# Half of the first layer's output product as seven block products instead of eight, with the weight sums formed by transfers

## The chip, the cores and the metric

The kernel runs on one core of one Trainium2 chip. The metric is device time in microseconds (us): the time of one execution, median of several runs. Each kernel was also executed once under the hardware profiler, and all instruction times below come from that one execution.

The engines are named as the profile names them. PE is the matrix engine and PEld its load of the stationary operand; DVE and ACT are the vector and scalar engines; POOL is the general engine, which here issues some transfers and does a little arithmetic; SP issues most transfers. Each engine works through its own instructions strictly in program order.

## The reference

Four residual layers over 256 tokens of width 1024, in float32. Layers 0 and 3 are of kind A, layer 1 of kind B (attention), layer 2 of kind C (pooling). Layer 0 is what the change touches:

```python
h = rms_norm(x, norm_gain[i])
proj = h @ w_in                      # 1024 -> 3 * 2048
u, v, z = proj[..., :2048], rms_norm(proj[..., 2048:4096], v_gain), proj[..., 4096:]
mixed = einsum('gij,bcjgd->bcigd', tril(w_s), v) + b_s   # 128-token chunks, 8 groups
y = u * mixed * silu(z)              # 256 x 2048
x = x + y @ w_out                    # 2048 -> 1024, the output product
```

The change concerns the first 1024 rows of `w_out`, and with them the first 1024 columns of `y`, in layer 0 alone.

## The kernel before

**Precision.** Every float32 operand is split in a high part, rounded to the format that PE takes at full rate, and the low rest. A product is three matmuls (`mm3`, lines 87 to 89): high by high, high by low, low by high, added up in one PSUM bank. The high part is made by ACT (`hi_of`, L92), the low part by DVE (`lo_of`, L95).

**Weights.** All weights lie in DRAM as one stream of units in the order of use. A unit is 256 rows by 512 columns, 512 KB. Unit u is loaded by SP (`load_units`, L177) into a raw buffer, split by ACT and DVE into one of seven pairs of buffers (`W_BUFS = 7`), and used by PE. There are four raw buffers of the tag `wr`; in the last layer `wx`, `wy` and `xs` serve as three more (`raw_place`). A raw buffer can be loaded again when the low part of its unit has been made.

**The order by hand.** `step(kk)` stands behind each half of a unit. It calls `tick()`, which runs the small tasks that are due, and then places the splitting of the unit five ahead (`AHEAD = 5`): the high part at the first half (kk = 0), the low part at the second (kk = 1). So a task that falls due at kk = 0 is placed ahead of the next ACT split, and one that falls due at kk = 1 ahead of the next DVE split. A tick has no time of its own: it sets only the order in each engine's program. What holds an engine up are the waits for data and for buffers.

**Layer 0.** Units 0 to 15 give v (four stages of 512 columns), units 16 to 47 alternate z and u (z0, u0, ..., z3, u3, four units each), units 48 to 63 are the output product `wo`. After each u stage `y_task` multiplies on DVE (`sz` L669, `yy` L674); two and four ticks later PE transposes the two token halves (`yp`, L682) through a single PSUM buffer, ACT and DVE split them (`y00h`, `y00l` and so on). The output product (`proj_out`) keeps four accumulators, two token halves t by two column halves n. One unit meets both token halves: 12 matmuls of 512 columns. At the end DVE adds the accumulators to `x` (L551).

**PSUM.** The big products take banks in turn from a ring of four (`pp`); a bank can be written again when its last reader is done.

**Seven products in layer 3.** For three of its four z/u pairs, layer 3 already replaces eight products of 512x512 blocks by seven (Strassen's scheme in Winograd's form). Each block product is 4 k-tiles by three matmuls with 128 tokens; its two units serve one token half only, so a unit gives 6 matmuls instead of 12. The sums of weight quarters are made in DRAM by POOL's transfers (`sums_of_quarters`, L188 for copies, L186 for adding ones; 16 transfers of 512 KB for one block), 19 of them placed in layer 0, 16 in layer 1 and 13 in layer 2 (`JOBS`). The sums of the activations' quarters are made on DVE and ACT (`sums_task`, L699 and L704) early in layer 3.

Of the kernel before, what the change touches and what calls it, by code (L numbers as in the profile page):

```python
# [10 lines left out]
F32 = mybir.dt.float32  # L11
# [3 lines left out]
ALU = mybir.AluOpType  # L15
PSUM = bass.MemoryType.PSUM

P = 128
# [25 lines left out]
LAST_AHEAD = 3  # L44
WARM = 17
FILL = 4
SEVEN = (0, 2, 3)
JOBS = (19, 16)


@with_exitstack
def hybrid_trunk_kernel(ctx, tc, x, wts, norm_gainT, a_v_gain, a_wsT, a_bsT, b_gl, b_gv, c_scaleT,
# [89 lines left out]


    seq = list(range(n_units))
    sums = {(n, j): dp.tile([4, P, UNIT], F32, name=f"sums{n}{j}") for n in SEVEN for j in range(2)}

    def seven_units(n):

        return n_units - 48 + 8 * n + (8 if n == 3 else 0)

    for n in reversed(SEVEN):
        z = seven_units(n)
        seq[z:z + 8] = [e[j] for e in (((n, 0, 0), (n, 0, 1)), (z, z + 1), (z + 6, z + 7), ((n, 3, 0), (n, 3, 1)),
                                       (z + 2, z + 3), ((n, 2, 0), (n, 2, 1)), ((n, 1, 0), (n, 1, 1)))
                        for j in range(2)]
    n_seq = len(seq)

    raw_users = {"wr": [-1] * RAW_BUFS, "xs": [-1], "wx": [-1], "wy": [-1]}

    def raw_place(i):  # L160

        return ("wr", "wr", "wx", "wr", "wy", "wr", "xs")[i % 7] if i >= n_units - 48 else "wr"

    def load_free():

# [22 lines left out]
                nc.gpsimd.dma_start(dst, src, max_dma_last_dim=UNIT)  # L188
            yield every

    def sum_jobs(n):

        z = seven_units(n)
        both = range(2)
        jobs = [(sums[n, j][i], wts[z + 2 * q + j], add) for i, q, add in
                ((0, 0, False), (2, 2, False), (0, 2, True), (2, 3, True)) for j in both]
        jobs += [(sums[n, j][3], sums[n, j][0], False) for j in both]
        jobs += [(sums[n, j][1], wts[z + 2 + j], False) for j in both]  # L200
        jobs += [(sums[n, j][3], wts[z + 6 + j], True) for j in both]
        jobs += [(sums[n, j][1], sums[n, j][3], True) for j in both]
        return jobs

    def split_hi(n):
# [316 lines left out]
    def proj_out(layer, nkt, yT, k0=0):  # L522


        acc = [[[(slice(0, HALF), pp(f"wo{layer}_{t}{n}"))] for n in range(2)] for t in range(2)]
        if layer == DEPTH - 1:

            acc[1][1] = [(slice(0, S), acc[1][1][0][1][:, :S]), (slice(S, HALF), atp(f"wo{layer}_b")[:, :S])]
        jt = (nkt - TAIL) // 2
        for j in range(k0 // 2, jt):  # L530
            for n in range(2):
                w = next_unit()
                for kk in range(2):
                    k = 2 * j + kk
                    for t in range(2):
                        for cs, o in acc[t][n]:
                            mm3(o, yT(k, t), (w[0][:, kk, cs], w[1][:, kk, cs]), k == k0, False)
                    step(kk, AHEAD if nkt == 16 else LAST_AHEAD)
        tail = [(j, n, next_unit()) for j in range(jt, nkt // 2) for n in range(2)]
        if nkt == 16:  # L540
            tail.sort(key=lambda e: e[1])
        ss = [tiny(2, f"ss{layer}_{t}") for t in range(2)]
        for t in range(2):
            for i, (j, n, w) in enumerate(tail):
                for cs, o in acc[t][n]:
                    for kk in range(2):
                        k = 2 * j + kk
                        mm3(o, yT(k, t), (w[0][:, kk, cs], w[1][:, kk, cs]), False, k == nkt - 1)
# [22 lines left out]
                tick()  # L571


    def load_a(layer, j):
# [13 lines left out]
    def layer_a(layer, consts, pl, mid):  # L588
# [98 lines left out]
                    yield 1  # L687
            done.add(("y", layer, n))


        if layer == DEPTH - 1:
            smh, sml = pair(pl, [P, 4, 4, P], "sm", f"sm{layer}", 1)

        def sums_task():
            q = {}
            for k, t in ((1, 1), (0, 1), (0, 0), (1, 0)):
                d = q[k, t] = tmp("sz", f"sq{layer}{k}{t}", 4).rearrange("p (k c) -> p k c", c=P)
                hh, hl = (a[:, 4 * k:4 * k + 4, t * P:(t + 1) * P].bitcast(F32) for a in hcur)
                nc.vector.tensor_tensor(d, hh, hl, op=ALU.add)  # L699
                yield 1  # L700
            a11, a12, a21, a22 = q[0, 0], q[1, 0], q[0, 1], q[1, 1]
            for i, (d, a, b, op) in enumerate(((a22, a21, a22, ALU.subtract), (a21, a11, a21, ALU.subtract),
                                               (a11, a22, a11, ALU.subtract), (a12, a12, a11, ALU.add))):
                nc.vector.tensor_tensor(d, a, b, op=op)  # L704
                hi_of(smh[:, i], d)
                yield 1
                lo_of(sml[:, i], d, smh[:, i])
                yield 1
            done.add(("sums", layer))

        S_A21_A22, S_A11_A21, S_REST, S_A12_REST = range(4)

        def seven_products(n):

            need(("sums", layer))

            def sm(i):
                return lambda k: (smh[:, i, k], sml[:, i, k])

            def product(o, a, first):  # L720
                for j in range(2):
                    w = next_unit()
                    for kk in range(2):
                        k = 2 * j + kk
                        mm3(o, a(k), (w[0][:, kk], w[1][:, kk]), first and k == 0, k == 3)
                        step(kk, due=kk == 1)

            def minus(o, name):
                d = tmp("vv", name, 2)
# [50 lines left out]
        for n in range(4):  # L780
            spawn(v_task(n, first if first and n == 0 else
                         proj_tok(f"v{layer}{n}", skew=layer if n == 0 else None)))
            if layer == DEPTH - 1 and n == 0:
                spawn(sums_task(), 4)
        def get(k, t):
            need(("y", layer, k // 4))
            sl = slice(t * P, (t + 1) * P)
            return yT[k // 4][0][:, k % 4, sl], yT[k // 4][1][:, k % 4, sl]

        if layer == 0:  # L790
            spawn(sums_of_quarters(jobs[:JOBS[0]], 4, 6))
        for n in range(4):
            if layer == DEPTH - 1 and n == 3:
                proj_half(layer, KT, get)
            if layer == DEPTH - 1 and n in SEVEN:
# [12 lines left out]


    def load_b():  # L810
# [20 lines left out]
    def layer_b(layer, consts, pl):  # L831
# [215 lines left out]
        for hp in range(NHEAD // 2):  # L1047
            for g in range(NG):
                spawn(qk_task(hp, g, proj_tok(f"qk{hp}{g}", skew=layer if hp == 0 and g == 0 else None)))
                if hp == 0 and g == 0:  # L1050
                    spawn(sums_of_quarters(jobs[JOBS[0]:sum(JOBS)], 10, 5))
                    gate(0)
                    gate(1)
            o = proj_tok(f"v01{hp}")
# [24 lines left out]
    def layer_c(layer, pl):  # L1079
# [103 lines left out]

        a, b, c, d = C_ORDER
        spawn(gate_tok(a, proj_tok(f"cz{a}", skew=layer)))
        spawn(sums_of_quarters(jobs[sum(JOBS):], 7, 4))
# [19 lines left out]


    box = {}
    jobs = [e for n in SEVEN for e in sum_jobs(n)]

    def after_ws():
        spawn(load_b())
# [36 lines left out]
def _weight_stream(a_w_in, a_w_out, b_w_in, b_w_out, c_w_in, c_w_grp, c_w_out):  # L1249
    parts = []  # L1250

    def layer_a(j):
        w = a_w_in[j]
        for n in range(4):
            parts.append(_units(w[:, 2048 + n * HALF:2048 + (n + 1) * HALF]))
        out_units = _out_units(a_w_out[j])
        for n in range(4):
            if j == 1 and n == 3:
                parts.append(out_units[:8])
# [105 lines left out]
```

## Time and profile before

| what | value |
|---|---|
| median of 3 runs | 828.72 us (828.41 to 828.74) |
| the profiled execution's own time | 828.51 us |
| its span, first to last instruction | 826.8 us |
| PE busy | 821.1 us (99%) |
| DVE busy | 581.4 us (70%) |
| ACT busy | 514.9 us (62%) |
| POOL busy | 83.5 us (10%) |
| moved by transfers | 184.21 MB, mean 223 GB/s |

The span is 1.7 us shorter than the execution's time; the rest lies before the first and after the last instruction. Busy time counts an engine from start to end of its instructions, overlaps once. A matmul's end is modelled, so its price is read from the distance between two starts. In the rows of the timeline the first number is the start, the second the duration, both in us, then engine, line, operation, written and read names, shape and count; in square brackets the idle time before and what ended it.

### The profile page before, as it was taken

Reading aid. Unit: us, or ns where it says so; the run is one execution under the profiler, and the core shown is the slowest. Engines: PE = TensorE matmul, PEld = TensorE weight load, DVE = VectorE, ACT = ScalarE, POOL = GpSimd, SP = SyncE. Lnnn points to the kernel's source line nnn. Section 1 sums busy time; section 2 is a strip of 40 time slices with the busy share of each in tenths; the row PEclk is TensorE's granted clock in tenths of the full one; section 3 lists DMA queues with packets and bytes.
Section 4 is the critical chain, followed back from the end, with each engine's and each line's share of the span. In section 5 each row is a group of like instructions: output and inputs, shape, how many; then the busy total and the mean of one; then the engine's idle time right before and its main releaser. Section 6 shows DMA issues by size and latency. Waiting matters only on the chain.

```text
span 826.8 us, 12566 instructions
## 1 busy us (share of the span) xinstructions
PE 821.1 (99%) x4585; PEld 711.4 (86%) x4585; DVE 581.4 (70%) x958; ACT 514.9 (62%) x947; POOL 83.5 (10%) x117
## 2 busy tenths in 40 slices
PE   9999999999999999999999999999999999999998
PEld 7888888888988888888888889999988888888887
DVE  5876656646657667667668576897864799979692
ACT  7775444436668687688688567546643668656560
POOL 1113120000201021021011014020000000000000
PEclk9999999999999999999999999999999999999999
DMA  8879999562968357369447269999665378868661
GB/s 281 305 241 311 322 319 300 176 197 84 288 201 228 125 194 242 125 164 250 147 149 257 78 200 280 291 279 278 231 227 178 103 244 303 289 213 324 200 234 52
DMA packets 60895, 184.21 MB, mean 223 GB/s; under 512 B 5952, under 2 KB 19024, under 8 KB 60704
## 3 DMA queue, kind: packets, MB, share of 16 engines
q1 hardware_dynamic: 43440, 154.16, 53.9%
q0 software_dynamic: 17104, 28.96, 15.4%
q8 instruction: 36, 0.59, 0.3%
q10 hardware_dynamic: 288, 0.28, 0.1%
q14 instruction: 27, 0.22, 0.1%
HBM read 182.32 MB, written 26.21 MB: 252 GB/s over the span
## 4 chain that ended last, share of the span: by engine, by line
PE 97%; DVE 1%; DMA 1%; ACT 1%; issue 0%; POOL 0%; ACTq 0%
PE qk L87 5%; PE qk L89 5%; PE qk L88 5%; PE wo L87 5%; PE wo L89 5%; PE wo L88 5%; PE v L87 5%; PE v L89 5%; PE v L88 5%; PE z L89 2%; PE z L87 2%; PE u L87 2%; PE u L88 2%; PE z L88 2%; PE u L89 2%; PE cz L89 2%
## 5 line engine op out<-in xcount | busy, mean ns | idle before, releaser
L854 POOL TENSOR_TENSOR qr<-qm,m 128x8 f32<-128x8 f32 x12 | 19.9, 1658 | 215.4 <-DVE qm L853 215.4
L849 ACT ACTIVATE junk<-qk 128x128 bf16<-128x128 f32 x96 | 26.6, 277 | 7.3 <-PE qk L89 4.7
L858 ACT ACTIVATE qn<-qk,qr 128x128 f32<-128x128 f32 x96 | 27.5, 381 | 3.6 <-POOL qr L854 3.6
L307 POOL TENSOR_TENSOR r<-ms,m 128x1 f32<-128x1 f32 x6 | 4.3, 710 | 198.5 <-DVE ms L304 198.5
L325 ACT ACTIVATE hT<-hp,gT 128x128 fp32r<-128x128 f32 x48 | 13.0, 383 | 15.0 <-PE hp L321 15.0
L186 POOL DMA_DIRECT2D sums<-in_wts_dram x18 | 19.3, 1205 | 24.1 <-DMA sums<-in_wts_dram 13.1
L853 DVE TENSOR_SCALAR qm<-qs 128x8 f32<-128x8 f32 x12 | 2.1, 172 | 26.7 <-ACT junk L849 26.7
L551 DVE TENSOR_TENSOR x<-wo,x 128x512 f32<-128x512 f32 (+1 forms) x16 | 10.8, 672 | 13.4 <-PE wo L89 13.3
L849 ACT ACTIVATION_READ_ACCUMULATOR junk<-qk 128x1 f32 x96 | 18.9, 197 | 0.0
L330 DVE SCALAR_TENSOR_TENSOR hT<-hp,gT,hT 128x128 fp32r<-128x128 f32 x48 | 13.5, 343 | 7.4 <-ACT hT L325 7.4
L299 ACT ACTIVATE junk<-x 128x512 bf16<-128x512 f32 x16 | 10.2, 639 | 10.1 <-DVE x L551 9.9
L948 ACT ACTIVATE p<-p,rl 128x384 f32<-128x384 f32 (+1 forms) x16 | 11.5, 769 | 4.8 <-DVE rl L947 4.8
L879 PE MATMUL qt<-ident,qn 128*128 128x128 f32 x96 | 14.4, 272 | 0.0
L871 DVE TENSOR_TENSOR rb<-qn,kcb 128x32 f32<-128x32 f32 x96 | 13.7, 184 | 0.0
L879 PEld LDWEIGHTS qt<-ident,qn 128*128 128x128 f32 x96 | 11.7, 140 | 2.3
L607 DVE TENSOR_TENSOR vv<-v,kc 128x512 f32<-128x512 f32 x16 | 10.7, 686 | 4.0 <-ACT junk L605 3.7
L669 DVE SCALAR_TENSOR_TENSOR sz<-u,m,sz 128x512 f32<-128x512 f32 x8 | 6.0, 746 | 10.3 <-PE u L89 10.3
L944 ACT ACTIVATE p<-p,nb 128x768 f32<-128x768 f32 x8 | 7.5, 937 | 7.6 <-DVE nb L943 7.6
L188 POOL DMA_DIRECT2D sums<-in_wts_dram x18 | 12.1, 716 | 0.3 <-issue 0.3
L867 DVE TENSOR_TENSOR ra<-qn,kcb 128x64 f32<-128x64 f32 x48 | 10.6, 220 | 1.1 <-ACT qn L858 0.4
L626 POOL TENSOR_TENSOR vr<-vme,m 128x1 f32<-128x1 f32 x4 | 2.8, 716 | 73.5 <-DVE vms L622 73.5
L979 PE MATMUL pt<-ident,p 128*128 128x128 f32 x48 | 9.9, 274 | 0.0
(2965 smaller groups left out, 3359.3 us busy)
## 6 DMA issues: line engine op xcount, KB each, us to landing
wr<-in_wts_dram SPq DMA_DIRECT2D x251, 512.0 KB, 4.6
sums<-in_wts_dram POOLq DMA_DIRECT2D x36, 512.0 KB, 11.8
wr<-sums SPq DMA_DIRECT2D x19, 512.0 KB, 4.6
sums<-sums POOLq DMA_DIRECT2D x12, 512.0 KB, 8.5
wx<-in_wts_dram SPq DMA_DIRECT2D x7, 512.0 KB, 5.1
wy<-in_wts_dram SPq DMA_DIRECT2D x7, 512.0 KB, 5.3
wx<-sums SPq DMA_DIRECT2D x3, 512.0 KB, 5.4
kc<-in_a_wsT_dram POOLq DMA_DIRECT2D x2, 512.0 KB, 7.6
```

The source lines that it names most:

```text
L87: nc.tensor.matmul(out_ap, lh[0], rh[0], start=start, stop=False, skip_group_check=True)
L88: nc.tensor.matmul(out_ap, lh[0], rh[1], start=False, stop=False, skip_group_check=True)
L89: nc.tensor.matmul(out_ap, lh[1], rh[0], start=False, stop=stop, skip_group_check=True)
L186: nc.gpsimd.dma_start(dst, src, accum_op=ALU.add, max_dma_last_dim=UNIT)
L188: nc.gpsimd.dma_start(dst, src, max_dma_last_dim=UNIT)
L325: nc.scalar.activation(h_parts(layer)[0][:, k, t * P:(t + 1) * P], pt[:, k % 4], AF.Copy, scale=gT[:, layer, k:k + 1])
L330: nc.vector.scalar_tensor_tensor(hTl, pt[:, k % 4], gT[:, layer, k:k + 1], hTh.bitcast(F32), op0=ALU.mult, op1=ALU.subtract)
L849: nc.scalar.activation(junk[:, :HD], ov[t][:, h], AF.Square, accum_out=ssq[t][:, h:h + 1])
L854: nc.gpsimd.tensor_tensor(rqs, ms, m05_row[:, :8], op=ALU.pow)
L858: nc.scalar.activation(qn[t][:, h], ov[t][:, h], AF.Copy, scale=rq[t][:, h:h + 1])
L871: nc.vector.tensor_tensor(rb[:, hs, s0:s0 + 16], qn[t][:, hs, s1:s1 + 16], c, op=ALU.mult)
L879: nc.tensor.transpose(pts[t][:, h], qn[t][:, h], ident)
```

## The change

In layer 0, rows 0 to 1023 of `w_out` (old units 48 to 55) are multiplied as seven block products: y's columns 0 to 511 and 512 to 1023 by two token halves on one side, four 512x512 quarters of weights on the other. `proj_seven` makes them; `proj_out` then does rows 1024 to 2047 as before.

- **Weight stream.** The eight units become fourteen: three quarters as they are and four sums, two units each. The sums are 16 more transfers on POOL, now 64 in all. They start behind v0 instead of behind v3, the first 16 for the output product. `JOBS` puts 20 into layer 0 (one every 4 ticks), 24 into layer 1 (every 7 instead of 10), 20 into layer 2 (every 5 instead of 7).
- **Raw buffers.** For these fourteen units `wx`, `wy` and `xs` join the four `wr` buffers.
- **Sums of y.** `y_sums` is started at z2 and works when y0 and y1 are finished: four additions of high and low part on DVE, then four times a subtraction or addition (DVE), a high part (ACT) and a low part (DVE). Its temporary tiles lie in `wx` and `wy`.
- **Adding to x.** Each of the seven products is added to x straight from its bank by DVE: eight additions of 128x512, since one bank is added twice. Two banks go on accumulating after they were read.
- **Ticks.** `part_product` ticks once per unit, at kk = 1.

Layer 3's seven products are the same in other functions' words (`left_sums`, `part_product`, `sum_tile` are its old inner functions moved out).

```diff
-SEVEN = (0, 2, 3)
-JOBS = (19, 16)
+BLOCKS = {("wo", 0): 48, ("zu", 0): -48, ("zu", 2): -32, ("zu", 3): -16}
+JOBS = (20, 24)
...
+        quarters = [(z, z + 1), (z + 2, z + 3), (z + 6, z + 7)] + [((b, i, 0), (b, i, 1)) for i in range(4)]
+        order = (3, 0, 2, 6, 1, 5, 4) if b[0] == "zu" else (0, 1, 3, 6, 2, 5, 4)
+        seq[z:z + 8] = [quarters[q][j] for q in order for j in range(2)]
...
+        return ("wr", "wr", "xs", "wr", "wr", "wx", "wy")[(i - out_raw) % 7] if out_raw <= i < out_raw + 14 else "wr"
...
+    def left_sums(name, quarter, place, smh, sml, key):
+        q = {}
+        for k, t in ((1, 1), (0, 1), (0, 0), (1, 0)):
+            d = q[k, t] = place(f"sq{name}{k}{t}").rearrange("p (k c) -> p k c", c=P)
+            hh, hl = (a.bitcast(F32) for a in quarter(k, t))
+            nc.vector.tensor_tensor(d, hh, hl, op=ALU.add)
+            yield 1
+        a11, a12, a21, a22 = q[0, 0], q[1, 0], q[0, 1], q[1, 1]
+        for i, (d, a, b, op) in enumerate(((a22, a21, a22, ALU.subtract), (a21, a11, a21, ALU.subtract),
+                                           (a11, a22, a11, ALU.subtract), (a12, a12, a11, ALU.add))):
+            nc.vector.tensor_tensor(d, a, b, op=op)
+            hi_of(smh[:, i], d)
+            yield 1
+            lo_of(sml[:, i], d, smh[:, i])
+            yield 1
+        done.add(key)
+
+    def part_product(o, a, first):
+        for j in range(2):
+            w = next_unit()
+            for kk in range(2):
+                k = 2 * j + kk
+                mm3(o, a(k), (w[0][:, kk], w[1][:, kk]), first and k == 0, k == 3)
+                step(kk, due=kk == 1)
...
+    def proj_seven(layer, yT, smh, sml):
+        def add(t, n, o, op=ALU.add):
+            xh = xt[t][:, n * HALF:(n + 1) * HALF]
+            nc.vector.tensor_tensor(xh, xh, o, op=op)
+            yield 1
...
+        xb = pp(f"xw{layer}")
+        part_product(xb, quarter(0, 0), True)
+        spawn(add(0, 0, xb), 1)
+        yb = pp(f"yw{layer}")
+        part_product(yb, quarter(1, 0), True)
+        spawn(add(0, 0, yb), 1)
+        need(("sums", layer))
+        zb = pp(f"zw{layer}")
+        part_product(zb, sum_tile(smh, sml, S_A21_A22), True)
+        spawn(add(1, 1, zb), 1)
+        part_product(xb, sum_tile(smh, sml, S_REST), False)
+        spawn(add(0, 1, xb, ALU.subtract), 1)
+        part_product(zb, sum_tile(smh, sml, S_A12_REST), False)
+        spawn(add(0, 1, zb), 1)
+        part_product(xb, sum_tile(smh, sml, S_A11_A21), False)
+        spawn(add(1, 1, xb, ALU.subtract), 1)
+        spawn(add(1, 0, xb), 1)
+        wb = pp(f"ww{layer}")
+        part_product(wb, quarter(1, 1), True)
+        spawn(add(1, 0, wb), 1)
...
+            if layer == 0 and n == 0:
+                spawn(sums_of_quarters(jobs[:JOBS[0]], 4, 10))
...
-        if layer == 0:
-            spawn(sums_of_quarters(jobs[:JOBS[0]], 4, 6))
+        def y_sums():
+            while ("y", layer, 1) not in done:
+                yield 1
+            room = [wx[:, 0], wx[:, 1], wy[:, 0], wy[:, 1]]
...
+            yield from left_sums(layer, y_quarter, place, smh, sml, ("sums", layer))
         for n in range(4):
+            if n == 2 and ("wo", layer) in BLOCKS:
+                spawn(y_sums(), 4)
...
-        proj_out(layer, 16, get, KT if layer == DEPTH - 1 else 0)
+        if ("wo", layer) in BLOCKS:
+            proj_seven(layer, get, smh, sml)
+        proj_out(layer, 16, get, KT if layer == DEPTH - 1 or ("wo", layer) in BLOCKS else 0)
```

More of the change, by code (lines that the diff above doesn't have):

```diff
@@ L144, in hybrid_trunk_kernel, with first_of @@
     seq = list(range(n_units))
[L145 to L155, printed above, removed]
+    sums = {(b, j): dp.tile([4, P, UNIT], F32, name=f"sums{b[0]}{b[1]}{j}") for b in BLOCKS for j in range(2)}
+    def first_of(b):
+        return BLOCKS[b] % n_units
+    for b in sorted(BLOCKS, key=first_of, reverse=True):
+        z = first_of(b)
+        quarters = [(z, z + 1), (z + 2, z + 3), (z + 6, z + 7)] + [((b, i, 0), (b, i, 1)) for i in range(4)]
+        order = (3, 0, 2, 6, 1, 5, 4) if b[0] == "zu" else (0, 1, 3, 6, 2, 5, 4)
+        seq[z:z + 8] = [quarters[q][j] for q in order for j in range(2)]
     n_seq = len(seq)
+    more_raw = seq.index((("zu", 0), 0, 0))
+    out_raw = first_of(("wo", 0))
     raw_users = {"wr": [-1] * RAW_BUFS, "xs": [-1], "wx": [-1], "wy": [-1]}
     def raw_place(i):
-        return ("wr", "wr", "wx", "wr", "wy", "wr", "xs")[i % 7] if i >= n_units - 48 else "wr"
+        if i >= more_raw:
+            return ("wr", "wr", "wx", "wr", "wy", "wr", "xs")[(i - more_raw) % 7]
+        return ("wr", "wr", "xs", "wr", "wr", "wx", "wy")[(i - out_raw) % 7] if out_raw <= i < out_raw + 14 else "wr"
     def load_free():
@@ L189, in sums_of_quarters, with sum_jobs @@
             yield every
-    def sum_jobs(n):
-        z = seven_units(n)
+    def sum_jobs(b):
+        z = first_of(b)
         both = range(2)
-        jobs = [(sums[n, j][i], wts[z + 2 * q + j], add) for i, q, add in
+        jobs = [(sums[b, j][i], wts[z + 2 * q + j], add) for i, q, add in
                 ((0, 0, False), (2, 2, False), (0, 2, True), (2, 3, True)) for j in both]
[L199 to L202, printed above, removed]
+        jobs += [(sums[b, j][3], sums[b, j][0], False) for j in both]
+        jobs += [(sums[b, j][1], wts[z + 2 + j], False) for j in both]
+        jobs += [(sums[b, j][3], wts[z + 6 + j], True) for j in both]
+        jobs += [(sums[b, j][1], sums[b, j][3], True) for j in both]
         return jobs
@@ L522, in proj_out, with bank @@
     def proj_out(layer, nkt, yT, k0=0):
-        acc = [[[(slice(0, HALF), pp(f"wo{layer}_{t}{n}"))] for n in range(2)] for t in range(2)]
+        acc = [[[], []], [[], []]]
+        def bank(t, n):
+            if not acc[t][n]:
+                acc[t][n].append((slice(0, HALF), pp(f"wo{layer}_{t}{n}")))
+        if ("wo", layer) not in BLOCKS:
+            for t in range(2):
+                for n in range(2):
+                    bank(t, n)
         if layer == DEPTH - 1:
@@ L535, in proj_out @@
                     for t in range(2):
+                        bank(t, n)
                         for cs, o in acc[t][n]:
@@ L571, in proj_out @@
                 tick()
+    S_A21_A22, S_A11_A21, S_REST, S_A12_REST = range(4)
+    def left_sums(name, quarter, place, smh, sml, key):
[14 more added lines that the diff above has]
+        done.add(key)
@@ new lines, in part_product, with sum_tile, quarter @@
+    def part_product(o, a, first):
[5 more added lines that the diff above has]
+                step(kk, due=kk == 1)
+    def sum_tile(smh, sml, i):
+        return lambda k: (smh[:, i, k], sml[:, i, k])
+    def proj_seven(layer, yT, smh, sml):
[3 more added lines that the diff above has]
+            yield 1
+        def quarter(k, t):
+            return lambda i: yT(4 * k + i, t)
+        xb = pp(f"xw{layer}")
[18 more added lines that the diff above has]
+        spawn(add(1, 0, wb), 1)
@@ L688, in y_task, with h_quarter @@
             done.add(("y", layer, n))
-        if layer == DEPTH - 1:
+        if layer == DEPTH - 1 or ("wo", layer) in BLOCKS:
             smh, sml = pair(pl, [P, 4, 4, P], "sm", f"sm{layer}", 1)
[L694 to L711, printed above, removed]
+        def h_quarter(k, t):
+            return (a[:, 4 * k:4 * k + 4, t * P:(t + 1) * P] for a in hcur)
         def seven_products(n):
@@ L717, in sm @@
             def sm(i):
[L718 to L726, printed above, removed]
+                return sum_tile(smh, sml, i)
+            product = part_product
             def minus(o, name):
@@ L782, in layer_a @@
                          proj_tok(f"v{layer}{n}", skew=layer if n == 0 else None)))
+            if layer == 0 and n == 0:
+                spawn(sums_of_quarters(jobs[:JOBS[0]], 4, 10))
             if layer == DEPTH - 1 and n == 0:
-                spawn(sums_task(), 4)
+                spawn(left_sums(layer, h_quarter, lambda n: tmp("sz", n, 4), smh, sml, ("sums", layer)), 4)
         def get(k, t):
@@ L788, in get, with place, y_quarter @@
             return yT[k // 4][0][:, k % 4, sl], yT[k // 4][1][:, k % 4, sl]
-        if layer == 0:
-            spawn(sums_of_quarters(jobs[:JOBS[0]], 4, 6))
+        def y_sums():
+            while ("y", layer, 1) not in done:
+                yield 1
+            room = [wx[:, 0], wx[:, 1], wy[:, 0], wy[:, 1]]
+            def place(name):
+                return room.pop()
+            def y_quarter(k, t):
+                return (a[:, :, t * P:(t + 1) * P] for a in yT[k])
+            yield from left_sums(layer, y_quarter, place, smh, sml, ("sums", layer))
         for n in range(4):
+            if n == 2 and ("wo", layer) in BLOCKS:
+                spawn(y_sums(), 4)
             if layer == DEPTH - 1 and n == 3:
                 proj_half(layer, KT, get)
-            if layer == DEPTH - 1 and n in SEVEN:
+            if layer == DEPTH - 1 and ("zu", n) in BLOCKS:
                 seven_products(n)
@@ L1050, in layer_b @@
                 if hp == 0 and g == 0:
-                    spawn(sums_of_quarters(jobs[JOBS[0]:sum(JOBS)], 10, 5))
+                    spawn(sums_of_quarters(jobs[JOBS[0]:sum(JOBS)], 7, 5))
                     gate(0)
@@ L1185, in layer_c @@
         spawn(gate_tok(a, proj_tok(f"cz{a}", skew=layer)))
-        spawn(sums_of_quarters(jobs[sum(JOBS):], 7, 4))
+        spawn(sums_of_quarters(jobs[sum(JOBS):], 5, 4))
         spawn(gate_feat(b, proj_feat(f"cz{b}")))
@@ L1208, in hybrid_trunk_kernel @@
     box = {}
-    jobs = [e for n in SEVEN for e in sum_jobs(n)]
+    jobs = [e for b in BLOCKS for e in sum_jobs(b)]
     def after_ws():
@@ L1256, in layer_a @@
         out_units = _out_units(a_w_out[j])
+        if j == 0:
+            out_units = np.concatenate([out_units[0:8:2], out_units[1:8:2], out_units[8:]])
         for n in range(4):
```

## The prediction

> **What bounds the kernel now.** I read the page first: span, busy shares, slices, chain of waits.
>
> ```profile
> span 826.8 us, 12566 instructions
> ...
> PE 821.1 (99%) x4585; PEld 711.4 (86%) x4585; DVE 581.4 (70%) x958; ACT 514.9 (62%) x947; POOL 83.5 (10%) x117
> ...
> PE   9999999999999999999999999999999999999998
> ...
> PEclk9999999999999999999999999999999999999999
> ...
> PE 97%; DVE 1%; DMA 1%; ACT 1%; issue 0%; POOL 0%; ACTq 0%
> ```
>
> PE sets the end everywhere: it is busy for nine tenths or more of every slice but the last, at the full granted clock, and carries 97% of the chain. So a matmul that goes away is worth its whole distance to the next, and any wait that the change gives PE costs its whole length. There is no idle time on PE to hide one in. Next I read PE's own timeline in the output product and in the second block of seven products in layer 3, for prices.
>
> ```profile
> 147.45 0.39 PE L87 MATMUL wo<-w48h,y00h 128*128 128x512 f32 x1
> ...
> 150.18 0.60 PE L682 MATMUL yp<-ident,yy 128*128 128x128 f32 x4
> ...
> 153.39 0.60 PE L682 MATMUL yp<-ident,yy 128*128 128x128 f32 x4
> ...
> 159.30 0.39 PE L87 MATMUL wo<-w52h,y01h 128*128 128x512 f32 x1
> ...
> 162.02 0.39 PE L87 MATMUL wo<-w53h,y01h 128*128 128x512 f32 x1
> ```
>
> Twelve matmuls, one unit, take 162.02 - 159.30 = 2.72 us: 0.227 us each. With four transposes among them they take 153.39 - 150.18 = 3.21 us, so the transposes cost 0.49.
>
> ```profile
> 735.33 0.39 PE L87 MATMUL zb<-w246h,sm3h 128*128 128x512 f32 x1
> ...
> 752.62 0.28 PE L87 MATMUL mx<-v32h,wsr30h 128*128 128x256 f32 x1
> ...
> 754.05 0.40 PE L87 MATMUL wb<-w258h,hT 128*128 128x512 f32 x1
> ...
> 756.79 0.39 PE L87 MATMUL wh<-w260h,y30h 128*128 128x512 f32 x1
> ```
>
> Block two of layer 3 has the load that the change brings to layer 0: fourteen units of six matmuls, with two groups of transposes. It takes 756.79 - 735.33 = 21.46 us, of which the mixing products take 754.05 - 752.62 = 1.43: 20.03 remain. Worked out, 14 x 1.36 + 2 x 0.49 = 20.02. So there PE never waited, though ACT, DVE and the loads handled a unit every 1.36 us instead of every 2.72. This is the change's best witness. The question is what differs in layer 0.
>
> **What is removed.** Eight units of 12 matmuls are 96; seven products of 12 are 84. Twelve go: 12 x 0.227 = **2.72 us** off the path. The transposes, mixing and v, z, u products stay.
>
> **What DVE gets in the seven products.** In layer 3 the banks that are used again are copied away by ACT, and DVE adds later. Here DVE reads every bank, eight times, and PE may not write a bank again before. DVE's prices:
>
> ```profile
> 146.97 0.75 DVE L669 SCALAR_TENSOR_TENSOR sz<-u,m,sz 128x512 f32<-128x512 f32 x1 [3.90 <-PE u L89]
> ...
> 150.12 1.22 DVE L95 TENSOR_TENSOR w53l<-wr,w53h 128x1024 fp32r<-128x1024 f32 x1
> ...
> 749.46 1.22 DVE L95 TENSOR_TENSOR w260l<-wr,w260h 128x1024 fp32r<-128x1024 f32 x1
> 750.60 0.68 DVE L758 TENSOR_TENSOR p<-yb,p 128x512 f32<-128x512 f32 x1
> 751.20 1.22 DVE L95 TENSOR_TENSOR w261l<-wx,w261h 128x1024 fp32r<-128x1024 f32 x1
> ```
>
> From start to start a low part takes 1.14 us and a half-size operation, here one that reads a bank, 0.60. Let T be PE's start of the output product, 147.45 now. DVE multiplies y3 until 150.12, T + 2.67, as before. Then its program holds, up to the last addition from the bank `xw`, which `wo0_00` takes next from the ring: the low parts of twelve units (the sixth to the seventeenth, five ahead of PE), two of y3, and seven additions. That is 12 x 1.14 + 9 x 0.60 = 19.1 us, with 0.14 for the last one's tail and the signal: T + 21.9. PE without a wait would be there at T + 20.0. The difference, **1.9 us**, has to be waited for; it falls on the second use of `zw` (some 0.9) and on `wo0_00` (some 0.9). Work ahead does not help: an addition stands behind the low part of the unit five ahead. Then the last addition (`ww`) stands behind two more low parts. The second of them waits for a load that starts when the fifteenth unit's low part is made and lands 4.6 us later (median, below): 25.6 against PE's 25.3, **0.3 us**. Bounds for both together: 0 if DVE's program were shorter than I count, since its block in layer 3 cost PE nothing; 6.8 us if one of the loads behind takes the longest landing, 10.7 (quoted with the transfers), 6.1 over the median, of which its low part's place in DVE's program hides some 1.5. I take 2.2, since all its prices have rows.
>
> [...]
>
> **The sums of y.** They fall into the end of z2 and into u2.
>
> ```profile
> 106.28 0.69 DVE L95 TENSOR_TENSOR y01l<-yp,y01h 128x512 fp32r<-128x512 f32 x1 [1.04 <-ACT y01h L92]
> ...
> 122.78 0.75 DVE L669 SCALAR_TENSOR_TENSOR sz<-u,m,sz 128x512 f32<-128x512 f32 x1 [3.01 <-PE u L89]
> ...
> 124.36 0.74 DVE L669 SCALAR_TENSOR_TENSOR sz<-u,m,sz 128x512 f32<-128x512 f32 x1
> ```
> ```profile
> 125.99 0.60 PE L682 MATMUL yp<-ident,yy 128*128 128x128 f32 x4
> ```
> ```profile
> 668.75 0.68 DVE L704 TENSOR_TENSOR sq<-sq,sq 128x512 f32<-128x512 f32 x1
> 669.35 1.22 DVE L95 TENSOR_TENSOR w220l<-wr,w220h 128x1024 fp32r<-128x1024 f32 x1
> ```
> ```profile
> 673.64 0.61 ACT L92 ACTIVATE sm3h<-sq 128x512 fp32r<-128x512 f32 x1
> 674.16 1.04 ACT L92 ACTIVATE w222h<-wr 128x1024 fp32r<-128x1024 f32 x1
> ```
>
> By amount there is room: twelve operations of 0.60 and six low parts of 1.14 are 14.0 us, and DVE has 122.78 - 106.28 = 16.5. But the order is bad. Counting ticks from z2's start, y1 is done at the fifth, the four additions stand at ticks 5 to 8, the subtractions at 9, 11, 13 and 15. Odd ticks are kk = 0, so a subtraction's high part stands on ACT ahead of the next unit's high part, and its low part on DVE ahead of that unit's low part. Layer 3 starts on an even tick: there the low part of unit 220 comes right behind the subtraction, as its row shows. In layer 0 each round is a chain: subtraction 0.68, ACT 0.52, ACT's unit 1.04, DVE's unit 1.14, three handovers of about 0.03: 3.46 us, against 2.72 of PE per unit. It begins at 106.28 + 5 x 0.60 + 2 x 1.14 = 111.6 and after four rounds is at 125.4, when y2's multiplication should have begun at 122.78. The transposes need its first half 1.58 us after its start (124.36 - 122.78) and 0.14 for tail and signal: 127.1, where they now start at 125.99. **1.1 us**, and 0.1 at the second transposes, whose buffer the late DVE frees late. Bounds: 0 (the work fits by amount) and 2.6 (the whole delay). I take 1.2, by the rows.
>
> **Transfers.**
>
> ```profile
> wr<-in_wts_dram SPq DMA_DIRECT2D x251, 512.0 KB, 4.6
> sums<-in_wts_dram POOLq DMA_DIRECT2D x36, 512.0 KB, 11.8
> ```
> ```profile
> 27.87 3.00 POOL L584 TENSOR_SCALAR_AFFINE_SELECT kc<-kc 128x128 f32<-128x128 f32 x8 [7.02 <-DMA kc<-in_a_wsT_dram]
> ...
> 56.77 0.56 POOL L626 TENSOR_TENSOR vr<-vme,m 128x1 f32<-128x1 f32 x1 [25.91 <-DVE vms L622]
> ...
> 121.17 2.29 POOL L188 DMA_DIRECT2D sums<-in_wts_dram  x3
> ```
>
> POOL is idle from 30.9 to 56.8. Four copies now start at about 31, the fifth transfer when the first has landed (11.8 us, 43), well before `vr`. The rest runs on from 65, as it does now until 121.17, with a head start of six; so all 16 sums are there by about 105, and the loads that need them come after 130. At the output product no sums are moved any more. The first seven of the fourteen units are loaded before T; each later load starts when the unit that held its buffer has its low part, and by the order above has 6 us or more until its own is due, but for the one named. In layers 1 and 2 a job comes every 7 or 5 ticks; a job that waits there stands ahead of POOL's small powers and clears, but dependent jobs lie two to four apart, and by their order no waiting pair lies just ahead of a power in layer 1. I take 0; the cover is PE's lead of five units, 13.6 us.
>
> **Sum.** -2.72 + 1.9 + 0.3 + 1.2 = +0.7 us on the profiled execution's 828.51 us (span 826.8): 829.2; the median of the runs is 0.2 above that execution. Forecast **829.3 us**, own range 828.3 to 830.3.
>
> **Rivals.**
> (a) DVE's waits stay hidden. For it: layer 3's blocks at the same pace. Against: there ACT frees the banks. 828.72 - 2.72 = 826.0. Chance 0.2.
> (b) One of the two waits comes, the other not: 829.3 - 2.2 = 827.1 or 829.3 - 1.2 = 828.1. For it: they have different causes. Chance 0.15.
> (c) Slower: the early copies starve the loads of v.
>
> ```profile
> 28.30 1.06 ACT L92 ACTIVATE w9h<-wr 128x1024 fp32r<-128x1024 f32 x1 [3.15 <-DMA wr<-in_wts_dram]
> ```
> ```profile
> 43.51 0.39 PE L87 MATMUL v<-w13h,hT 128*128 128x512 f32 x1
> ```
> ```profile
> DMA to landing us min/median/max: 3.1/4.6/10.7
> ```
> ```profile
> DMA to landing us min/median/max: 6.7/13.1/26.7
> ```
>
> The last two rows are the loads of units to `wr` and the adding transfers (L186). ACT is waiting for loads there already. Unit 13's load starts when unit 9 is split, 28.30 + 1.06 + 1.22 = 30.6, with the copies. Splitting takes 2.3 us, so it must land by 41.2: 10.6 us. If it takes what an adding transfer takes in the median, 13.1, PE waits 2.5 us: 831.8. Against: the longest load of `wr` took 10.7. Chance 0.13.
>
> **How the numbers follow.** Forecast 0.52, (a) 0.2, (b) 0.15, (c) 0.13. A difference under 0.2%, 1.66 us, can't be told from no change: faster is below 827.1, slower above 830.4. Faster holds (a) and a little of (b), 0.23; slower holds (c) and the forecast's tail, 0.17; within, 0.6. The range takes in (a) and goes up to 831.0, which leaves out most of (c).
>
> **What would show it.** The output product of layer 0 with 84 + 96 matmuls; DVE without a gap from T + 2.7 to T + 22; PE idle ahead of the second `zw` product and of `wo0_00`, released by DVE's additions to x; in u2 subtraction, ACT, ACT, DVE in turn, and PE idle ahead of y2's transposes. If PE shows no idle time at these places, (a) is right and my reading of the order wrong; idle time at `v` with ACT waiting for loads would be (c).

## The result and the profile after

The change makes the kernel slower: 834.18 us (median of 6 runs, 831.21 to 834.98) against 828.62 us (6 runs, 828.41 to 828.74), a ratio of 1.0062 with a 95% interval of 1.0048 to 1.0077. The forecast was 829.3 us and no measurable change. The measured time lies 3.9 us above the range stated beside it (828.3 to 830.3), and 3.2 above 831.0, where the wider range given with the chances ends. The profiled execution took 834.12 us, its span 832.4 us, 5.6 more than before.

The page of the kernel after: span, busy time by engine, the chain of waits.

```profile
span 832.4 us, 12625 instructions
...
PE 822.4 (99%) x4573; PEld 710.1 (85%) x4573; DVE 600.7 (72%) x984; ACT 523.9 (63%) x957; POOL 97.6 (12%) x133
...
PE 89%; DVE 4%; ACT 3%; issue 2%; DMA 2%; POOL 0%; ACTq 0%; DVEq 0%
```

PE has 12 instructions less, as forecast, and yet more busy time: some matmuls took longer. PE's share of the chain fell from 97% to 89%; DVE, ACT and transfers stand in it now. The waits of PE in the kernel after (waiting line, releaser, us in total, times, the longest) name two new places, `yp` and `zw`; the one of `zw`, 0.7 us, is quoted with PE's rows below:

```profile
PE yp L765 <- DVE yy L757: 3.7, 2, 2.9
```

The rows of PE's timeline where z1 and u1 begin, first before, then after, place the loss.

```profile
74.89 0.39 PE L87 MATMUL z<-w24h,hT 128*128 128x512 f32 x1
...
86.74 0.39 PE L87 MATMUL u<-w28h,hT 128*128 128x512 f32 x1
```

```profile
75.18 0.39 PE L89 MATMUL z<-w24h,hT 128*128 128x512 f32 x1
...
77.67 0.39 PE L91 MATMUL z<-w24h,hT 128*128 128x512 f32 x1
80.95 0.74 PE L765 MATMUL yp<-ident,yy 128*128 128x128 f32 x4 [2.89 <-DVE yy L757]
81.44 0.54 PE L89 MATMUL z<-w25h,hT 128*128 128x512 f32 x1
...
82.21 0.63 PE L91 MATMUL z<-w25h,hT 128*128 128x512 f32 x1
...
85.17 0.39 PE L89 MATMUL z<-w25h,hT 128*128 128x512 f32 x1
...
91.77 0.39 PE L89 MATMUL u<-w28h,hT 128*128 128x512 f32 x1
```

From z1 to u1 PE needed 11.85 us before and 16.59 after: **4.74 us** of the 5.6 are lost in this one stage. 3.05 are the gap ahead of y0's transposes (80.95 - 77.67 less one matmul, 0.23). The rest is a slow clock: from 81.44 to 85.17 nine matmuls took 3.73 us where nine at 0.227 are 2.04, so **1.69**; most stand 0.43 apart, and the granted clock there is 0.50 instead of 1.00. From z3 to u3 1.5 us are lost, from the output product's start to layer 1 1.3 won; another 0.7 is spread over the rest.

Why y0 was late shows in ACT's timeline, before and after:

```profile
40.01 1.06 ACT L92 ACTIVATE w16h<-wr 128x1024 fp32r<-128x1024 f32 x1 [0.55 <-DMA wr<-in_wts_dram]
...
72.69 1.06 ACT L92 ACTIVATE w28h<-wr 128x1024 fp32r<-128x1024 f32 x1 [4.98 <-DMA wr<-in_wts_dram]
```

```profile
42.13 1.06 ACT L94 ACTIVATE w14h<-wr 128x1024 fp32r<-128x1024 f32 x1 [4.28 <-DMA wr<-in_wts_dram]
...
47.00 1.06 ACT L94 ACTIVATE w16h<-wr 128x1024 fp32r<-128x1024 f32 x1 [1.32 <-PE v L91]
...
77.30 1.06 ACT L94 ACTIVATE w28h<-wr 128x1024 fp32r<-128x1024 f32 x1 [1.79 <-DMA wr<-in_wts_dram]
```

The splitting of unit 16 came 7.0 us later than before, that of unit 28 4.6 us later, both behind loads. (The row of unit 16 names PE, but PE had done with unit 9, whose pair of buffers unit 16 takes, at 35.6; the rows of units 14 and 28 name the transfers.) POOL's timeline of after shows what moved at those times:

```profile
30.05 2.51 POOL L195 DMA_DIRECT2D sumswo<-in_wts_dram  x4
70.48 2.17 POOL L193 DMA_DIRECT2D sumswo<-in_wts_dram  x2
```

A load of a unit issued between 25 and 50 us landed after 5.1 us (median) before and after 7.0 now; these are the rows of the transfers in that window, before and after:

```profile
wr<-in_wts_dram SPq DMA_DIRECT2D x14, 512.0 KB, 5.1
```

```profile
wr<-in_wts_dram SPq DMA_DIRECT2D x11, 512.0 KB, 7.0
sumswo<-in_wts_dram POOLq DMA_DIRECT2D x5, 512.0 KB, 10.4
```

And DVE's timeline, before and after, carries the lateness to y0:

```profile
62.92 1.22 DVE L95 TENSOR_TENSOR w24l<-wr,w24h 128x1024 fp32r<-128x1024 f32 x1
...
73.79 1.23 DVE L95 TENSOR_TENSOR w28l<-wr,w28h 128x1024 fp32r<-128x1024 f32 x1 [4.44 <-ACT w28h L92]
74.93 0.74 DVE L669 SCALAR_TENSOR_TENSOR sz<-u,m,sz 128x512 f32<-128x512 f32 x1
```

```profile
67.87 1.22 DVE L97 TENSOR_TENSOR w24l<-wr,w24h 128x1024 fp32r<-128x1024 f32 x1
...
78.39 1.23 DVE L97 TENSOR_TENSOR w28l<-wr,w28h 128x1024 fp32r<-128x1024 f32 x1 [1.62 <-ACT w28h L94]
79.53 0.75 DVE L752 SCALAR_TENSOR_TENSOR sz<-u,m,sz 128x512 f32<-128x512 f32 x1
```

The multiplication of y0 stands in DVE's program right behind the low part of unit 28, which PE needs only four units later, and it was held there: PE's last matmul of u0 ended at 75.34, DVE then stood idle for the 1.62 us ahead of that low part, and `sz` came behind it at 79.53. Both come 4.60 us later. The transposes follow `sz` by 1.42 us (79.53 to 80.95), so before the change they could have begun at 76.35, and PE came to them at 77.61: 1.26 us were slack. PE itself came 0.29 later now; the other 3.05 reach PE.

The lateness comes from v and not from the transfers near y0. Unit 28 is loaded into the raw buffer of unit 24, whose low part was made 4.95 us later than before (67.87 against 62.92), ahead of the transfers from 70.48 on: of the 7.0 us at unit 16 only 2 were won back. From the end of that low part to ACT's start on unit 28 it took 8.55 us before and 8.21 after, so unit 28's load itself did not become slower. The kernel before has transfers beside this load too.

At y2 the forecast chain is there, in DVE's timeline of after:

```profile
116.70 0.69 DVE L605 TENSOR_TENSOR wy<-wy 128x512 f32<-128x512 f32 x1
...
119.03 1.23 DVE L97 TENSOR_TENSOR w41l<-wr,w41h 128x1024 fp32r<-128x1024 f32 x1 [0.26 <-ACT w41h L94]
120.18 0.69 DVE L605 TENSOR_TENSOR wy<-wx,wy 128x512 f32<-128x512 f32 x1
```

A round takes 120.18 - 116.70 = 3.48 us (forecast 3.46), and PE waits at both transposes of y2, 1.01 and 0.27 us. In the seven products PE's timeline has one wait of weight, DVE's timeline its cause; the stretch 160 to 180 in windows (length, then busy time of PE, PEld, DVE, ACT, POOL) shows how full DVE is:

```profile
166.63 0.47 PE L89 MATMUL zw<-w56h,sm0h 128*128 128x512 f32 x1 [0.69 <-DVE x L629]
...
175.06 0.39 PE L89 MATMUL wo<-w62h,y02h 128*128 128x512 f32 x1
```

```profile
165.80 0.68 DVE L629 TENSOR_TENSOR x<-x,zw 128x512 f32<-128x512 f32 x1
...
174.41 1.27 DVE L629 TENSOR_TENSOR x<-x,xw 128x512 f32<-128x512 f32 x2
```

```profile
160.00:180.00 20.00, 19.31 (x86) 15.21 (x85) 19.78 (x22) 12.51 (x13) 0.00 (x0) 1.00 0.77 249
```

The second `zw` product started 0.85 us late, the first matmul into the fourth bank of `wo` 0.15. But `wo0_00` started at 175.06 without a gap, while DVE's two additions from `xw` ran until 175.68.

### The profile page after: what moved, and what is told of

It reads as the page before. It is cut to its first block, busy times and chain, and to the rows that moved or that the text cites. A ratio compares the mean times of both kernels' runs of the same rounds, so it can differ in the third digit from the quotient of the medians.

```text
span 832.4 us, 12625 instructions
## 1 busy us (share of the span) xinstructions
PE 822.4 (99%) x4573; PEld 710.1 (85%) x4573; DVE 600.7 (72%) x984; ACT 523.9 (63%) x957; POOL 97.6 (12%) x133
## 4 chain that ended last, share of the span: by engine, by line
PE 89%; DVE 4%; ACT 3%; issue 2%; DMA 2%; POOL 0%; ACTq 0%; DVEq 0%
PE qk L89 5%; PE qk L91 5%; PE qk L90 5%; PE v L91 5%; PE v L89 5%; PE v L90 5%; PE wo L89 4%; PE wo L91 4%; PE wo L90 4%; PE cz L89 2%; PE cz L91 2%; PE cz L90 2%; PE cx L90 2%; PE cx L91 2%; PE cx L89 2%
## 5 line engine op out<-in xcount | busy, mean ns | idle before, releaser
L193 POOL DMA_DIRECT2D sumszu<-in_wts_dram x18 | 19.2, 1212 | 11.9 <-DMA sumszu<-sumszu 9.1
L765 PE MATMUL yp<-ident,yy 128*128 128x128 f32 x64 | 10.0, 276 | 3.8 <-DVE yy L757 3.7
L195 POOL DMA_DIRECT2D sumszu<-in_wts_dram x18 | 13.5, 833 | 0.3 <-issue 0.3
L765 PEld LDWEIGHTS yp<-ident,yy 128*128 128x128 f32 x64 | 7.6, 140 | 6.9 <-issue 4.5
```

The lines of the kernel that those rows point to most:

```text
L193: nc.gpsimd.dma_start(dst, src, accum_op=ALU.add, max_dma_last_dim=UNIT)
L765: nc.tensor.transpose(pt[:, k], ys[t][:, k * P:(k + 1) * P], ident)
```

## The experiments

**1. The transfers alone.** The kernel before, with its own 19 transfers of layer 0 started behind v0 instead of behind v3; nothing else changed.

```diff
 (kernel before)
+            if layer == 0 and n == 0:
+                spawn(sums_of_quarters(jobs[:JOBS[0]], 4, 10))
-        if layer == 0:
-            spawn(sums_of_quarters(jobs[:JOBS[0]], 4, 6))
```

> The kernel before with one edit: its own 19 transfers of layer 0 start behind v0 (first after 10 ticks) instead of behind v3. No seven products in layer 0, no sums of y. Theory 1 (the early copies slow the loads of v's last units, use up PE's lead of five units, and the next group of transfers then makes PE wait ahead of y0's transposes): 831 to 834 us, PE idle some 3 us at y0's transposes around 78 us, and a lower granted clock behind that. Rival (the cause is the volume of the 16 added transfers or anything else of the new output product): 828.6 us, no idle time there.

Measured: 832.76 us (830.55 to 833.17), ratio 1.0043 (1.0028 to 1.0058) to the kernel before. Its profile, of the run of 830.55, has the wait at y0's transposes in PE's timeline:

```profile
79.21 0.74 PE L682 MATMUL yp<-ident,yy 128*128 128x128 f32 x4 [1.46 <-DVE yy L674]
```

The early transfers cost 4 us by themselves, with no seven products in layer 0. In this execution the gap was 1.62 us and the matmuls behind it kept their pace, 0.23 us apart. The three longer runs were not profiled; each lists a mean granted clock of 0.998 where the profiled one lists 1.000, as the kernel after does with its one slow stretch.

**2. All of the change but the early transfers.**

```diff
-            if layer == 0 and n == 0:
-                spawn(sums_of_quarters(jobs[:JOBS[0]], 4, 10))
+        if layer == 0:
+            spawn(sums_of_quarters(jobs[:JOBS[0]], 3, 6))
```

> The changed kernel with its 20 transfers of layer 0 started behind v3 again (after 6 ticks, one every 3), all else as changed. Theory 1: the wait at y0's transposes and the low clock behind it go, 4.8 us: 834.2 - 4.8 = 829.4 us; the waits at y2's transposes (1.3) and in the seven products (1) stay. Rival (volume): 833 us or more, the wait comes elsewhere in layer 0, or the loads of the sums come late at the output product.

Measured: 829.22 us (828.80 to 830.58, 10 runs), ratio 1.0009 (1.0000 to 1.0019). The waits of PE between 60 and 200 us:

```profile
PE yp L765 <- DVE yy L757: 0.9, 1, 0.9
PE zw L89 <- DVE x L629: 0.7, 1, 0.7
```

The wait at y0 is gone, with the slow matmuls; the ones at y2 and `zw` stay. The place of the transfers cost 5 us of the change's time. What is left comes out at the forecast, 829.3, but by luck: the terms as measured, -2.72 + 1.0 + 1.28, would give 828.3. The forecast's 1.2 us too much for the seven products stand in for 0.9 us that no term explains.

**3. One more tick ahead of the subtractions**, with the transfers early, so that the subtractions fall on even ticks.

```diff
 def y_sums():
             while ("y", layer, 1) not in done:
                 yield 1
+            yield 1
```

> The changed kernel with the sums of y started one tick later, so that each subtraction stands ahead of DVE's next unit and not of ACT's. Theory 2 (the order makes the wait at y2's transposes): PE idle ahead of y2's transposes falls from 1.3 us to under 0.2, time 834.2 - 1.3 = 832.9 us, the wait at y0 stays. Rival (the twelve operations are too much for DVE there): the wait stays within 0.3 us of what it is.

Measured: 834.68 us (832.60 to 838.80, 4 runs), ratio 1.0078 (1.0048 to 1.0108): no gain in time. The profile is that of the longest run, 838.80; the waits of PE:

```profile
PE yp L765 <- DVE yy L757: 3.7, 1, 3.7
...
PE wo L89 <- DVE cyy L1252: 3.1, 1, 3.1
```

Only one wait on `yp` is left, that of y0; z3 to u3 takes 11.8 us again, as before the change. The chain at y2 is therefore what the forecast says. But y0's gap was longer here, and a new one of 3.2 us stood in layer 2's output product, behind loads that came late beside that layer's transfers. Behind the two gaps matmuls stood 0.43 us apart, until 87.0 and from 612.7 to 616.1 us; the mean granted clock of this execution is 0.994, against 0.998 in the kernel after. With the transfers this close the time scatters by 6 us, and 1.3 can't be seen in it.

**4. Both edits**, the second and the third experiment's.

> Both edits: transfers behind v3 and the sums of y one tick later. Theories 1 and 2 together: 834.2 - 4.8 - 1.3 = 828.1 us, with about 1 us of waiting left in the seven products against 2.7 saved; if the two waits are the whole of the loss, 0.5 us or more below the kernel before is as far as it gets. Rival: some wait moves on, 829.5 us or more.

Measured: 827.69 us (827.39 to 829.95, 10 runs), ratio 0.9994 (0.9984 to 1.0003). In the profile only the waits at `zw` (0.84) and at `wo`'s fourth bank (0.16) are left in layer 0. Against experiment 2 the tick is worth 1.5 us, the size of y2's wait. Here the tick shows in the time.

**5. Room between two uses of a bank.** Experiment 4 with the product `ww` moved ahead of the second `zw` (and the units in that order), so that DVE has 2.7 us more for the addition from `zw`.

```diff
-order = ... else (0, 1, 3, 6, 2, 5, 4)
+order = ... else (0, 1, 3, 6, 4, 2, 5)
...
         spawn(add(0, 1, xb, ALU.subtract), 1)
+        wb = pp(f"ww{layer}")
+        part_product(wb, quarter(1, 1), True)
+        spawn(add(1, 0, wb), 1)
         part_product(zb, sum_tile(smh, sml, S_A12_REST), False)
```

> e4_both with the last product (bank ww) moved ahead of the second zw product, so that two products instead of one lie between the two uses of zw; weights in the new order. Theory 3 (what is left of the wait in the seven products is PE waiting for DVE's addition from zw, 0.85 us, for want of a product in between): PE idle there under 0.2 us, time 827.7 - 0.85 = 826.9 us. Rival (DVE is short of time over the whole stretch, so the wait moves to the next bank): the same idle time ahead of xw or of proj_out's first bank, 827.7 us.

Measured: 827.90 us (827.37 to 831.47, 11 runs), ratio 0.9995 (0.9985 to 1.0004). PE's timeline:

```profile
172.27 0.50 PE L89 MATMUL wo<-w63h,y02h 128*128 128x512 f32 x1 [1.11 <-DVE x L629]
```

The wait at `zw` is gone, and one of 1.27 us stands at a bank of `wo` in its place. The rival holds: the time did not fall, and the order only said who waits for DVE.

**6. Layer 2's transfers spread.** Experiment 4 with 28 transfers in layer 1 (every 6 ticks) and 16 in layer 2 (every 7).

```diff
-JOBS = (20, 24)
+JOBS = (20, 28)
```

> e4_both with layer 2's transfers as thin as before: 28 in layer 1 (one every 6 ticks), 16 in layer 2 (one every 7 instead of 20, one every 5). Theory 4 (executions of the late-start kernels that take 1 to 3 us longer do so because layer 2's denser transfers make units of its output product late): the slow ones of e4 (829.9 us) go, all within 827.3 to 828.0. Rival (the scatter is from layer 0): as many slow executions as in e4.

Measured: 827.61 us (827.21 to 829.21, 11 runs), ratio 0.9991 (0.9982 to 1.0000). The profile has no wait in layer 2, but experiment 4's had none either, and 4 of 11 runs still lie above 828.3, where the theory had all of them below 828.0; of experiment 4 it was 3 of 10. So the theory is not borne out. Whether the spreading does anything stays open, and so does the cause of the longer runs.

**7. The gap filled.** The change, with 27 matmuls of zeros (128x256, about 2.9 us, result unused) in PE's program ahead of y0's first transposes.

> The changed kernel with 27 small matmuls on zeros, 2.9 us of PE work, placed ahead of y0's first transposes, where PE idles 3 us; nothing else changed. Theory 5 (the lower granted clock behind that gap comes from PE's idleness): the matmuls behind the transposes keep 0.227 us and not 0.43, time 834.2 - 1.8 = 832.4 us or a little less. Rival (the clock falls for another reason, or the wait is on DVE and the filling delays PE further): 834 us or more, slow matmuls as before.

Measured: 834.97 us (832.82 to 837.37, 4 runs), ratio 1.0077 (1.0059 to 1.0096). PE's timeline of the profiled run, 832.82:

```profile
78.04 3.12 PE L766 MATMUL idle<-wx 128*128 128x256 bf16 x27
...
81.67 0.39 PE L90 MATMUL z<-w25l,hT 128*128 128x512 f32 x1
81.89 0.39 PE L91 MATMUL z<-w25h,hT 128*128 128x512 f32 x1
```

With PE kept busy no matmul is slow: the rows stand 0.22 apart at once, and z1 to u1 takes 14.8 us instead of 16.6. So the clock's part is shown in the trace. The median did not fall by it; in the scatter of this kernel 1.7 us is not settled by four runs.

**8. Only the first four copies early**, the other transfers behind v3.

```diff
-                spawn(sums_of_quarters(jobs[:JOBS[0]], 4, 10))
+                spawn(sums_of_quarters(jobs[:4], 4, 10))
...
+        if layer == 0:
+            spawn(sums_of_quarters(jobs[4:JOBS[0]], 3, 6))
```

> The changed kernel with only the first four transfers (plain copies) behind v0; the other sixteen start behind v3 (after 6 ticks, one every 3). Theory 1 (the four copies at 31 us alone use up the lead, by slowing the loads of units 13 to 16): PE still idles 1.5 us or more ahead of y0's transposes, 831 us or more. Rival (the adding transfers ahead of the next group, or their number after 64 us, do it): the wait falls under 0.5 us, 829.4 us as with all of them late.

Measured: 831.03 us (829.73 to 832.52, 6 runs), ratio 1.0032 (1.0020 to 1.0045), between experiment 2 and the change. PE's gap at y0 in its profile is 1.06 us, at full pace behind it. The copies, from 36.05 us in this profile, suffice by themselves to use up y0's slack. In the change the gap is 2.0 us longer. That difference stands at unit 24 already, which ACT splits at 64.15 here and at 66.20 in the change, ahead of the group of transfers at 70 to 78 us. Whether the fifth early transfer makes it, or the copies' start six us earlier there, stays open.

**9. Banks that need not wait for DVE.** Experiment 6, with the first reading of `zw` as a copy by ACT and its addition four ticks later, and two accumulators of `wo` in PSUM buffers of the mixing products.

```diff
-                acc[t][n].append((slice(0, HALF), pp(f"wo{layer}_{t}{n}")))
+                acc[t][n].append((slice(0, HALF), (atp if n and ("wo", layer) in BLOCKS else pp)(f"wo{layer}_{t}{n}")))
...
-        spawn(add(1, 1, zb), 1)
+        def keep_add():
+            d = tmp("sz", f"zk{layer}", 4)
+            nc.scalar.activation(d, zb, AF.Copy)
+            yield 4
+            xh = xt[1][:, HALF:]
+            nc.vector.tensor_tensor(xh, xh, d, op=ALU.add)
+            yield 1
+        spawn(keep_add(), 1)
```

> The kernel with the transfers behind v3, the extra tick, and layer 2's transfers spread, with two more edits: the first reading of the bank zw is a copy by ACT (the addition to x follows from the copy four ticks later), and two of the four accumulators of wo lie in PSUM buffers of the mixing products, so that only two come from the ring. Theory: the two waits left in the seven products (0.85 ahead of the second zw, 0.17 ahead of wo's fourth bank) are waits for DVE, which is short of time only over this stretch; with ACT freeing one bank and two banks taken elsewhere, DVE may run late without PE waiting, and both go: 827.6 - 1.0 = 826.6. Rival: the wait moves on once more, to the second xw product (whose bank DVE still reads first) or to the splitting of a unit, because DVE has as much to do as before: 827.6 again, with a wait of about 1 us at another place.

Measured: **826.45 us** (826.36 to 827.49, 10 runs), ratio 0.9974 (0.9965 to 0.9984): faster than both kernels. In PE's timeline of layer 0's output product one small gap is left:

```profile
161.85 0.39 PE L91 MATMUL zw<-w57h,sm0l 128*128 128x512 f32 x1
162.38 0.50 PE L89 MATMUL xw<-w58h,sm0h 128*128 128x512 f32 x1
```

0.30 us (0.53 less one matmul) ahead of the third `xw` product, which waits for DVE's subtraction from that bank (161.65 to 162.33): the kind of place the rival named, at a third of its price. DVE has as much to do as before; what it has not done when the seven products end, it does under the eight units behind them, where a low part is due only every 2.72 us. That PE could be freed of DVE by buffers, and not by order, is what sets this apart from experiment 5. Which of the two buffer edits gave how much was not tried apart.

**10. Gaps of three sizes.** Experiment 4 with y's first half made six, seven and eight times over by DVE ahead of y0, y1 and y2, so that PE's gaps grow.

```diff
+                if layer == 0 and t == 0:
+                    for _ in range((6, 7, 8, 0)[n]):
+                        nc.vector.tensor_tensor(y, up[t], us[t], op=ALU.mult)
```

> The kernel with the transfers behind v3 and the extra tick, whose PE has no wait at the transposes of y0, y1 and y2. DVE makes y's first half six, seven and eight times over ahead of y0, y1 and y2 (0.60 us each, into the same tile), so that PE should stand idle there for about 2.2, 2.8 and 3.4 us (the extra time less the 1.35 us by which the product was early). Nothing is left out. Theory: an idle gap of some length between 1.6 us (no loss seen) and 3.05 us (matmuls at 0.43 us for 3.7 us behind it) halves PE's rate: the gaps of 2.8 and 3.4 us are followed by matmuls 0.43 us apart for about 3.7 us, the gap of 2.2 us is open; each such stretch costs some 1.8 us beside the gap. Rival: the slow matmuls were not the gap's doing but that of whatever was late there (ACT and DVE behind loads): then all three gaps are followed by matmuls 0.227 us apart.

Measured: 840.96 us, one run. PE's timeline at the three gaps:

```profile
77.31 0.39 PE L91 MATMUL z<-w24h,hT 128*128 128x512 f32 x1
80.13 0.99 PE L768 MATMUL yp<-ident,yy 128*128 128x128 f32 x4 [2.44 <-DVE yy L760]
...
81.77 0.63 PE L91 MATMUL z<-w25h,hT 128*128 128x512 f32 x1
...
83.48 0.53 PE L89 MATMUL z<-w25h,hT 128*128 128x512 f32 x1
...
105.75 0.39 PE L91 MATMUL z<-w32h,hT 128*128 128x512 f32 x1
109.27 0.74 PE L768 MATMUL yp<-ident,yy 128*128 128x128 f32 x4 [3.13 <-DVE yy L760]
...
110.31 0.39 PE L91 MATMUL z<-w33h,hT 128*128 128x512 f32 x1
...
133.67 0.39 PE L91 MATMUL z<-w40h,hT 128*128 128x512 f32 x1
137.91 0.88 PE L768 MATMUL yp<-ident,yy 128*128 128x128 f32 x4 [3.86 <-DVE yy L760]
...
139.45 0.63 PE L91 MATMUL z<-w41h,hT 128*128 128x512 f32 x1
...
141.58 0.49 PE L90 MATMUL z<-w41l,hT 128*128 128x512 f32 x1
```

My theory, a length from which a gap slows PE, is wrong, and so is the rival: the gap of 2.6 us (start to start, less 0.23) was followed by slow matmuls, the one of 3.3 was not, the one of 4.0 was. What sets the three apart the runs do not show.

## Why the prediction was wrong, step by step

- **"So a matmul that goes away is worth its whole distance to the next, and any wait that the change gives PE costs its whole length."** Right. Experiment 9, with the waits gone but for 0.30, is 2.23 us below the kernel before; 2.72 less 0.30 would be 2.42. For the wait at y0 it was too little: 3.05 us of waiting cost 4.74.
- **The two waits in the seven products, 2.2.** Mis-sized: 1.0 (0.85 at the second `zw`, forecast 0.9; 0.15 at the last addition, forecast 0.3). The term that failed is "the bank `xw`, which `wo0_00` takes next from the ring", 0.9: `wo0_00` began while `xw` was still being read, so it had another bank. Banks were not taken strictly in turn; which one it took, the trace doesn't say. DVE's count behind the term was right: its additions from `xw` ended at T + 21.75 (175.68 - 153.93; forecast T + 21.9), and the windows show it busy for 19.78 of 20 us. The 0.3 had a wrong reason: no low part ahead of the last addition waited for a load (DVE's rows from 174.41 to 177.87 follow without a gap); DVE was simply full. The additions from banks stood 0.60 apart (162.93 to 163.53), as far as the subtraction from SBUF and what follows it (668.75 to 669.35 before).
- **The sums of y, 1.2.** Right in place, mechanism and size: 1.01 and 0.27, a round of 3.48 us for 3.46, and the tick of experiment 3 takes it away.
- **"I take 0; the cover is PE's lead of five units, 13.6 us."** This step failed, and it decided the result. The lead covers the units' splitting. It does not cover what stands behind a low part in DVE's program and is needed at once: y0's multiplication, whose slack was 1.26 us and not 13.6. The rows of before showed it, though I did not read them: ACT already waited 4.98 us for unit 28's load and DVE 4.44 for its high part, with `sz` directly behind. Lateness of that load beyond the slack was bound to reach PE. Moreover I put the transfers beside the loads as if they cost them nothing, since "the longest load of `wr` took 10.7"; but beside the copies the median load went from 5.1 to 7.0 us, and one late load after another adds up, to 7.0 us at unit 16. Experiment 1 has the price alone (+4.1), experiment 2 the change without it (-5.0).
- **Rival (c), 831.8, chance 0.13.** Its mechanism came, not its place. At v PE did not wait: there the lead did cover. The lost lead was not won back before y0. The transfers that stand beside the loads there did not add to it: loads issued between 64 and 80 us landed after 8.2 us (median) before the change and after 7.5 with it. (c) had also the wrong price, since it had one late load in it and no change of pace behind the gap.
- **The slow matmuls, 1.69 us,** were in no step. The first part's "at the full granted clock" described a PE that never stood still; a forecast with a gap in it has to ask what the pace is behind the gap.
- **The sum by the measured terms:** -2.72 + 1.0 + 1.28 = -0.4, and +4.74 at y0 make +4.3 of the span's +5.6. The rest lies in small pieces: 0.3 ahead of z1, which is there at unit 4 already (19.10 against 18.84), before any transfer was moved, 0.2 more at z3, 0.4 in the output product and 0.4 in layers 1 to 3; their causes stay open. The range failed because the transfers stood in the sum at 0, without an upper bound of their own; their only price, that of (c), came from one late load and lay outside the range.

## What to carry to other kernels

A lead of several units protects only what is read several units later; look in each engine's program for work that stands behind a load and is needed at once, and take its slack, not the lead, as the cover for a transfer that is moved. A wait in the rows of before that ends on a transfer marks where a later transfer can come through first. Where one engine is full over a stretch, moving its work about only moves the wait: another engine or a spare buffer has to take part of it.

## What the runs showed of the hardware

**The clock behind a gap.** PE's matmuls stood 0.43 instead of 0.227 us apart behind some gaps. In the kernel after, the granted clock was 0.50 from 81.69 to 85.10, for 3.41 us, and 1.00 before and behind. In experiment 10 its mean was 0.57 from 80.0 to 84.0 and 0.60 from 137.7 to 142.0, and 1.00 from 77.7 to 80.1, 84 to 88 and 142 to 146; at 0.50 in the slow part that makes 3.4 us each time, an estimate from the two means. The gaps ahead were 3.05 us (the kernel after), 2.6 and 4.0 (experiment 10). Behind gaps of 1.62 (experiment 1) and 3.3 (experiment 10) the pace stayed.

Experiment 3 has two more. Behind its gap of 3.8 us at y0 (77.79 to 81.60) matmuls were slow until 87.0, behind its gap of 3.2 us in layer 2 from 612.7 to 616.1. With the gap of the change filled (experiment 7) the pace stayed. So the standing idle made the difference there, but its length alone does not decide: 2.6 us were enough in one place and 3.3 were not in another. What decides beside it was not shown.

**The rate by format.** A matmul of 512 columns with split operands (fp32r) took 0.227 us. The 27 of experiment 7 in bf16, 256 columns each, stood 0.11 apart (78.04 to 81.00), 0.22 for 512. Four transposes in f32, 512 columns together, cost 0.49 (before).

**Copies in DRAM beside loads.** A copy or addition of 512 KB from DRAM to DRAM took 10.4 us (median) to land in the stretch quoted above, and a load of the same size issued in that stretch took 7.0 instead of 5.1.
